# DoRA forward kernel: row stores moved to ScalarE's DMA ring, with a small zero store ahead of them

## The chip, the cores and the metric

The kernel runs on one core of a Trainium2 chip. A core has engines that run side by side: TensorE (PE, matrix products; PEld is its loading of weights), VectorE (DVE), ScalarE (ACT), GpSimd (POOL) and SyncE (SP). Sixteen DMA engines move data between the chip's main memory and the core's on-chip memory. An engine of the core issues a transfer into a ring (a queue); SP has one ring and ACT has another, and both feed the same 16 DMA engines. Times are device microseconds (us) of one execution.

## What is computed

The reference builds one 256 x 256 weight matrix and multiplies 32,768 rows by it:

```
W_adapted = W + scale * (lora_A @ lora_B)
W_norm = np.sqrt(np.sum(W_adapted ** 2, axis=0, keepdims=True) + 1e-8)
W_final = (W_adapted / W_norm) * m
y = x.reshape(-1, 256) @ W_final
```

x has the shape (16, 2048, 256) in float32, 33.5 MB, and y is as large. The rank of lora_A and lora_B is 16. All of W, lora_A, lora_B and m is 289 KB.

## The kernel before

The rows are cut into 8 blocks of 4,096 rows (`BLK`, 4 MB each). A block lies in one buffer `x_sb` of 128 partitions, with 32 rows on each, so that every partition reads 32 KB in one piece. There are 5 such buffers (`XBUFS`).

First the small inputs are loaded: W (`w_nat`, L65) on SP's ring, and lora_A (`a_nat`, L63), lora_B (`b_nat`, L67) and m (`m_row`, L69) on ACT's ring. From them the final weights `w_final` are made in bfloat16 (L85 to L129) by a chain of short steps over PE, DVE and ACT.

Then each block goes through 8 groups of 4 rows per partition. In a group PE transposes the rows through the identity (L156, tile `xt_ps`), DVE casts the result to bfloat16 (L162, `xt_sb`), PE multiplies by `w_final` (L167, `y_ps`), and ACT copies the product back over the same rows of `x_sb` (L174). When the groups of a block are done, one store of 4 MB writes the block out (L179); the last block is stored in three parts, of 2, 1 and 1 MB (`store_after`).

All loads and stores of rows are issued by SP, in the order in which they are written in the code, because `manual_schedule` holds SP's order fixed. That order is: W, loads 0 to 4, store 0, store 1, load 5, store 2, load 6, store 3, load 7, stores 4 to 6, and the three parts of store 7. Load 5 goes into the buffer of block 0 and so waits until store 0 has landed; loads 6 and 7 wait for stores 1 and 2. A store waits for ACT's last copy of its block. As SP works its list in order, what stands behind a waiting transfer waits too, and on the ring the transfers are worked in the order of issue.

Of the kernel before, what the change touches and what calls it, by code (L numbers as in the profile page):

```python
# [11 lines left out]
def kernel(  # L12
# [10 lines left out]
    nc = tc.nc  # L23
    P = 128
    FP32 = mybir.dt.float32
# [9 lines left out]
    KC = IN // P  # L35
    J = 4
    DJ = 32
    XBUFS = 5
    BLK = DJ * P
    NBLK = N // BLK  # L40

# [1 line left out]

    consts = ctx.enter_context(tc.tile_pool(name="consts", bufs=1))
    startup = ctx.enter_context(tc.tile_pool(name="startup", bufs=1))
    xpool = ctx.enter_context(tc.tile_pool(name="xpool", bufs=XBUFS))
    xtpool = ctx.enter_context(tc.tile_pool(name="xtpool", bufs=2))
    pp_xt = ctx.enter_context(tc.tile_pool(name="pp_xt", bufs=2, space=bass.MemoryType.PSUM))
    pp_y = ctx.enter_context(tc.tile_pool(name="pp_y", bufs=2, space=bass.MemoryType.PSUM))
# [1 line left out]
    def load_x(b):  # L51
        t = xpool.tile([P, DJ, IN], FP32, name="x_sb", tag="x_sb")
        nc.sync.dma_start(
            out=t,
            in_=x_flat[b * BLK : (b + 1) * BLK].rearrange("(p j) k -> p j k", p=P),
        )
        return t

    ctx.enter_context(tc.manual_schedule(engines={mybir.EngineType.SP}))


    a_nat = startup.tile([P, KC, R], FP32)
    nc.scalar.dma_start(out=a_nat, in_=lora_A.rearrange("(c p) r -> p c r", p=P))  # L63
# [3 lines left out]
    nc.scalar.dma_start(out=b_nat, in_=lora_B)  # L67
    m_row = startup.tile([1, OUT], FP32)
    nc.scalar.dma_start(out=m_row, in_=m[None, :])  # L69

    identity = consts.tile([P, P], FP32)
    make_identity(nc, identity)
# [10 lines left out]
    with tc.high_priority():  # L83
# [15 lines left out]
        for c in range(KC):  # L99
# [10 lines left out]
            out=wa, in0=ab_ps, scalar=float(scale), in1=w_nat, op0=ALU.mult, op1=ALU.add  # L110
# [27 lines left out]
    store_after = [[CH] for _ in range(NBLK)]  # L138
    store_after[-1] = [CH // 2, 3 * CH // 4, CH]

    x_tiles = {}
    for b in range(XBUFS):
        x_tiles[b] = load_x(b)

    for b in range(NBLK):
        x_sb = x_tiles[b]
        j_stored = 0


        for c in range(DJ // J):
            xt_ps = pp_xt.tile([P, KC, J * P], FP32, tag="psxt", name="xt_ps")
            for j in range(J):
                for kc in range(KC):
                    nc.tensor.transpose(  # L156
                        xt_ps[:, kc, j * P : (j + 1) * P],
                        x_sb[:, c * J + j, kc * P : (kc + 1) * P],
                        identity,
                    )  # L160
            xt_sb = xtpool.tile([P, KC, J * P], BF16, name="xt_sb")
            nc.vector.tensor_copy(out=xt_sb, in_=xt_ps)  # L162

            y_ps = pp_y.tile([P, J, OUT], FP32, tag="psy", name="y_ps")
            for kc in range(KC):
                for j in j_order:
                    nc.tensor.matmul(  # L167
                        y_ps[:, j, :],
                        xt_sb[:, kc, j * P : (j + 1) * P],
                        w_final[:, kc, :],  # L170
                        start=(kc == 0 and (j % (J // 2)) == 0),
                        stop=(kc == KC - 1 and (j % (J // 2)) == (J // 2) - 1),
                    )
            nc.scalar.copy(out=x_sb[:, c * J : (c + 1) * J, :], in_=y_ps)  # L174

            if c + 1 in store_after[b]:
                j0 = j_stored
                j_stored = (c + 1) * J
                nc.sync.dma_start(  # L179
                    out=out_flat[b * BLK : (b + 1) * BLK].rearrange(  # L180
                        "(p j) k -> p j k", p=P
                    )[:, j0:j_stored, :],
                    in_=x_sb[:, j0:j_stored, :],
                )
        if b >= 1 and b - 1 + XBUFS < NBLK:
            x_tiles[b - 1 + XBUFS] = load_x(b - 1 + XBUFS)


# [33 lines left out]
```

## Time and profile before

| what | value |
|---|---|
| median of 4 runs | 165.67 us (165.36 to 165.73) |
| the profiled execution's own time | 165.29 us |
| its span (first to last instruction) | 163.5 us |
| busy: DVE cast L162 | 75.4 us, 64 of 1.219 us |
| busy: ACT copy L174 | 64.8 us, 64 of 1.013 us |
| 4 MB row loads, issue to landing (median of 8) | 29.5 us |
| 4 MB row stores, issue to landing (median of 7) | 28.5 us |
| main memory read and written | 33.85 MB and 33.55 MB, 412 GB/s over the span |

The profile is of one execution. Its busy table says how long each engine worked. A line of slices cuts the span into 40 equal parts and gives the busy share of each in tenths, 9 being 90% or more. The DMA part lists the rings by number (q1 is SP's, q10 is ACT's, q8 and q14 fetch instructions): packets, MB, and the time that their packets took as a share of 16 engines' span. A stretch line gives for a window of time each engine's busy us (and number of instructions), the clock that TensorE was granted, the DMA engines' busy share and the GB/s; as a packet counts where it starts, shares of a short window can go a little past 1. A line of waits reads "who <- for whom: us in total, times, longest". The chain of waits follows the last instruction back to what released it. Besides, the trace holds a record of each DMA packet: its start, its length and its ring; a 4 MB transfer is 128 packets of 32 KB, one for each partition, and 8 for each DMA engine.

### The profile page before, as it was taken

How to read it: one execution, taken by the hardware profiler on the slowest of the kernel's cores; microseconds unless marked ns; L12 is line 12 of the kernel's file. 1: busy time of each engine (PE TensorE's matmuls, PEld its weight loads, DVE VectorE, ACT ScalarE, POOL GpSimd, SP SyncE). 2: the span in 40 equal slices, each digit the busy share in tenths (PEclk: the TensorE clock that was granted, in tenths of full speed). 3: DMA queues.
4: the chain of work that ended last, by engine and by line, in shares of the span. 5: the costliest groups of instructions: out<-in, count | busy, mean ns of one | idle time of the engine just before them, and what ended most of it. 6: DMA issues, size and time to landing. Idle time of an engine off the chain costs nothing.

```text
span 163.5 us, 2378 instructions
## 1 busy us (share of the span) xinstructions
PE 123.7 (76%) x1034; PEld 108.0 (66%) x1034; DVE 81.1 (50%) x76; ACT 66.8 (41%) x67; POOL 0.7 (0%) x6
## 2 busy tenths in 40 slices
PE   0149788888888888888888888888888888884000
PEld 0028677777777777777777777777777777772000
DVE  0145755555555555555555555555555555551000
ACT  3001144444444444444444444444444444444000
POOL 1000000000000000000000000000000000000000
PEclk9999999999999999999999999999999999999755
DMA  6998998998999999999999999999999999999992
GB/s 196 429 473 385 457 441 381 489 409 385 493 401 361 401 469 417 427 449 413 433 433 409 477 409 417 433 427 421 441 425 457 421 417 441 425 421 429 405 407 106
DMA packets 3180, 67.55 MB, mean 413 GB/s; under 512 B 593, under 2 KB 866, under 8 KB 866
## 3 DMA queue, kind: packets, MB, share of 16 engines
q1 hardware_dynamic: 2864, 67.37, 96.8%
q8 instruction: 8, 0.13, 0.3%
q10 hardware_dynamic: 306, 0.03, 0.2%
q14 instruction: 2, 0.02, 0.0%
HBM read 33.85 MB, written 33.55 MB: 412 GB/s over the span
## 4 chain that ended last, share of the span: by engine, by line
PE 55%; DVE 26%; DMA 4%; issue 4%; ACT 1%; DVEq 1%; ACTq 1%
PE y_ps L167 35%; DVE xt_sb L162 23%; PE xt_ps L156 17%; DMA m_row<-in_m_dram 4%; PE n_ps L118 1%; DVE rnorm L127 1%; DVEq L217 1%; PE mb_ps L94 1%; ACT x_sb L174 1%; DVE w_final L129 0%; DVE sq L113 0%; DVE wa L109 0%; ACTq L63 0%; ACTq L67 0%; ACT norm L122 0%
## 5 line engine op out<-in xcount | busy, mean ns | idle before, releaser
L162 DVE CAST xt_sb<-xt_ps 128x1024 bf16<-128x1024 f32 x64 | 75.4, 1219 | 55.2 <-PE xt_ps L156 55.2
L174 ACT COPY x_sb<-y_ps 128x1024 f32<-128x1024 f32 x64 | 64.8, 1013 | 70.4 <-PE y_ps L167 69.8
L167 PE MATMUL y_ps<-w_final,xt_sb 128*128 128x256 bf16 x512 | 66.7, 273 | 15.3 <-DVE xt_sb L162 14.9
L156 PE MATMUL xt_ps<-identity,x_sb 128*128 128x128 f32 x512 | 67.2, 277 | 0.0
L167 PEld LDWEIGHTS <-xt_sb 128*128 128x128 bf16 x512 | 46.8, 98 | 28.3 <-DVE xt_sb L162 23.9
L156 PEld LDWEIGHTS xt_ps<-identity,x_sb 128*128 128x128 f32 x512 | 59.3, 144 | 1.0 <-DMA x_sb<-in_x_dram 0.3
L122 ACT ACTIVATE norm<-n_ps,eps_col 128x256 f32<-128x256 f32 x1 | 0.5, 474 | 10.5 <-PE n_ps L118 10.5
L94 PE MATMUL mb_ps<-m_row,ones 1*128 1x256 f32 x2 | 1.2, 694 | 4.5 <-DMA m_row<-in_m_dram 4.5
L94 PEld LDWEIGHTS mb_ps<-m_row,ones 1*128 1x128 f32 x2 | 0.5, 304 | 5.0 <-issue 5.0
L89 PE MATMUL aT_ps<-identity,a_nat 128*16 128x128 f32 x2 | 0.6, 397 | 4.0 <-DMA a_nat<-in_lora_A_dram 4.0
L118 PE MATMUL n_ps<-sq,ones 128*128 128x256 f32 x4 | 2.1, 674 | 1.5 <-DVE sq L113 1.5
L85 DVE CAST b_bf<-b_nat 16x256 bf16<-16x256 f32 x1 | 0.3, 281 | 5.6 <-DMA b_nat<-in_lora_B_dram 5.6
L127 DVE RECIPROCAL rnorm<-norm 128x256 f32<-128x256 f32 x1 | 1.8, 1755 | 2.0 <-ACT norm L122 2.0
L89 PEld LDWEIGHTS aT_ps<-identity,a_nat 128*16 128x16 f32 x2 | 0.1, 88 | 4.0 <-issue 4.0
L118 PEld LDWEIGHTS n_ps<-sq,ones 128*128 128x128 f32 x4 | 1.2, 324 | 2.2 <-DVE sq L113 2.0
L79 ACT ACT_TABLE_LOAD x1 | 1.3, 1283 | 2.3 <-issue 2.3
L96 DVE COPY m_all<-mb_ps 128x256 f32<-128x256 f32 x1 | 0.4, 426 | 3.1 <-PE mb_ps L94 3.1
L129 DVE TENSOR_TENSOR w_final<-wam,rnorm 128x256 bf16<-128x256 f32 x2 | 0.8, 421 | 0.0
L125 DVE TENSOR_TENSOR wam<-wa,m_all 128x256 f32<-128x256 f32 x2 | 0.8, 418 | 0.0
L113 DVE TENSOR_TENSOR sq<-wa 128x512 f32<-128x512 f32 x1 | 0.7, 692 | 0.0
L109 DVE SCALAR_TENSOR_TENSOR wa<-ab_ps,w_nat 128x512 f32<-128x512 f32 x1 | 0.7, 692 | 0.0
L100 PE MATMUL ab_ps<-b_bf,aT 16*128 16x256 bf16 x2 | 0.6, 416 | 0.0
(11 smaller groups left out, 2.0 us busy)
## 6 DMA issues: line engine op xcount, KB each, us to landing
x_sb<-in_x_dram SPq DMA_DIRECT2D x8, 4096.0 KB, 29.5
out_dram<-x_sb SPq DMA_DIRECT2D x7, 4096.0 KB, 28.5
out_dram<-x_sb SPq DMA_DIRECT2D x1, 2048.0 KB, 15.7
out_dram<-x_sb SPq DMA_DIRECT2D x2, 1024.0 KB, 12.5
w_nat<-in_W_dram SPq DMA_DIRECT2D x1, 256.0 KB, 3.0
a_nat<-in_lora_A_dram ACTq DMA_DIRECT2D x1, 16.0 KB, 3.1
b_nat<-in_lora_B_dram ACTq DMA_DIRECT2D x1, 16.0 KB, 5.3
m_row<-in_m_dram ACTq DMA_DIRECT2D x1, 1.0 KB
```

The lines of the kernel that those rows point to most:

```text
L79: nc.scalar.activation(out=warm, in_=eps_col, func=AF.Sqrt)
L89: nc.tensor.transpose(aT_ps[:, c * P : (c + 1) * P], a_nat[:, c, :], identity)
L94: nc.tensor.matmul(mb_ps, ones[0:1, :], m_row, start=True, stop=True)
L118: nc.tensor.matmul(n2_ps, ones, sq[:, c, :], start=(c == 0), stop=(c == KC - 1))
L125: nc.vector.tensor_mul(out=wam[:, c], in0=wa[:, c], in1=m_all)
L127: nc.vector.reciprocal(out=rnorm, in_=norm)
L129: nc.vector.tensor_mul(out=w_final[:, c], in0=wam[:, c], in1=rnorm)
L156: nc.tensor.transpose(xt_ps[:, kc, j * P : (j + 1) * P], x_sb[:, c * J + j, kc * P : (kc + 1) * P], identity,)
L162: nc.vector.tensor_copy(out=xt_sb, in_=xt_ps)
L167: nc.tensor.matmul(y_ps[:, j, :], xt_sb[:, kc, j * P : (j + 1) * P], w_final[:, kc, :], start=(kc == 0 and (j % (J // 2)) == 0), stop=(kc ...
L174: nc.scalar.copy(out=x_sb[:, c * J : (c + 1) * J, :], in_=y_ps)
L217: with _tile.TileContext(nc) as tc:
```

## The change

The row stores are issued by ACT instead of SP, so that they go to ACT's ring, and SP's ring holds W and the row loads alone. SP's order is no longer written out by hand: the loads stand in the block loop, and each is issued as soon as its buffer is free (there are 5 buffers, as before). A tile `mark` of 128 x 16 zeros is made by a DVE memset, and ACT stores it (8 KB, 64 bytes from each partition) to a scratch tensor in main memory, behind its three small loads. Nothing reads the scratch tensor.

```diff
-    ctx.enter_context(tc.manual_schedule(engines={mybir.EngineType.SP}))
...
     nc.scalar.dma_start(out=m_row, in_=m[None, :])
+    scratch = nc.dram_tensor("scratch", (P, 16), FP32, kind="Internal").ap()
+    mark = startup.tile([P, 16], FP32)
+    nc.vector.memset(mark, 0.0)
+    nc.scalar.dma_start(out=scratch, in_=mark)
...
-    x_tiles = {}
-    for b in range(XBUFS):
-        x_tiles[b] = load_x(b)
     for b in range(NBLK):
-        x_sb = x_tiles[b]
+        x_sb = load_x(b)
...
-                nc.sync.dma_start(
+                nc.scalar.dma_start(
                     out=out_flat[b * BLK : (b + 1) * BLK].rearrange(
                         "(p j) k -> p j k", p=P
                     )[:, j0:j_stored, :],
                     in_=x_sb[:, j0:j_stored, :],
                 )
-        if b >= 1 and b - 1 + XBUFS < NBLK:
-            x_tiles[b - 1 + XBUFS] = load_x(b - 1 + XBUFS)
```

More of the change, by code (lines that the diff above doesn't have):

```diff
@@ L37 @@
     DJ = 32
-    XBUFS = 5
     BLK = DJ * P
@@ L45 @@
     startup = ctx.enter_context(tc.tile_pool(name="startup", bufs=1))
-    xpool = ctx.enter_context(tc.tile_pool(name="xpool", bufs=XBUFS))
+    xpool = ctx.enter_context(tc.tile_pool(name="xpool", bufs=5))
     xtpool = ctx.enter_context(tc.tile_pool(name="xtpool", bufs=2))
```

## The prediction

> **What bounds the kernel now.** I read the busy table first, then the DMA part, the slices, the stretches, and last who waited for whom on the queue that issues.
>
> ```profile
> PE 123.7 (76%) x1034; PEld 108.0 (66%) x1034; DVE 81.1 (50%) x76; ACT 66.8 (41%) x67; POOL 0.7 (0%) x6
> ...
> DMA  6998998998999999999999999999999999999992
> ...
> q1 hardware_dynamic: 2864, 67.37, 96.8%
> q8 instruction: 8, 0.13, 0.3%
> q10 hardware_dynamic: 306, 0.03, 0.2%
> ```
>
> No compute engine is above 76%, while the 16 DMA engines are full from the first slice to the last. q1 is SyncE's ring (67.37 MB, 96.8% of 16 engines' span); q10 is ScalarE's, which today carries 0.03 MB. The chain of waits names PE and DVE, since it follows back from the last instruction, but that instruction is not the end of the work. The stretches show it (columns: PE, PEld, DVE, ACT, POOL busy, clock, DMA share, GB/s):
>
> ```profile
> 4.00:12.00 8.00, 2.20 (x6) 0.88 (x6) 2.27 (x5) 0.00 (x0) 0.00 (x0) 1.00 1.03 436
> ...
> 45.30:49.30 4.00, 3.56 (x33) 3.17 (x32) 2.36 (x2) 1.91 (x3) 0.00 (x0) 1.00 0.92 393
> 49.30:52.30 3.00, 2.55 (x24) 2.23 (x23) 2.11 (x2) 1.17 (x2) 0.00 (x0) 1.00 1.09 360
> 52.30:56.30 4.00, 3.55 (x34) 3.17 (x32) 2.24 (x3) 2.03 (x2) 0.00 (x0) 1.00 1.01 434
> ...
> 152.00:158.00 6.00, 0.00 (x0) 0.00 (x0) 0.00 (x0) 0.00 (x0) 0.00 (x0) 0.63 0.99 421
> 158.00:163.50 5.50, 0.00 (x0) 0.00 (x0) 0.00 (x0) 0.00 (x0) 0.00 (x0) 0.50 0.42 176
> ```
>
> After 152 us nothing computes and DMA still runs at 0.99. The last store is issued at about 150.1 us (ACT's last copy starts at 149.05 and takes 1.01) and lands 12.5 us later, at 162 us: it stands behind the ring's backlog. So the end is bytes over rate. The trace's packet records give the rate: each of the 1,920 packets of 32 KB has a median of 1.213 us, that is 27.0 GB/s for an engine, and on each engine the next starts where the last ends. A 4 MB transfer is 8 such packets on each engine, 9.7 us. The 16 engines finish between about 159.3 and 162.2 us; the last sets the end. The queue's own waits:
>
> ```profile
> SPq L179 <- ACT x_sb L174: 99.6, 10, 20.3
> SPq L53 <- DMA out_dram<-x_sb: 31.7, 3, 14.1
> ```
>
> SP waits 99.6 us for copies and 31.7 us for stores to free a buffer, but as the ring always held 10 us or more of earlier work, none of it left the engines idle.
>
> **The change, part by part.**
>
> 1. Bytes. 67.37 MB on q1 become about 33.8 MB on q1 and 33.55 MB on q10, plus 8 KB. On the same 16 engines that is the same 128 packets' worth of 1.213 us for each engine, 155.3 us. What is left to ask is whether an engine is ever idle, and whether a packet becomes longer.
>
> 2. Idle turns. Only SP's order changes: loads 5, 6 and 7 no longer stand behind stores 1, 2 and 3. The five first loads start at 3.1 us as before. Stores are issued as blocks end, by the records at 34.2, 50.7, 67.1, 83.6 and so on, 16.46 apart. By 34.2 some 26 of the 40 first load packets of an engine are through ((34.2 - 3.1) / 1.213). From then the rings share. If they take turns, a load and a store packet take 2.43 us, so store 0 ends at about 55, store 1 at 74, store 2 at 94, store 3 at 113; the 38 load packets left (14 and 24 of loads 5 to 7) end at 34.2 + 38 x 2.43 = 126.5. Load 5 may start at 56, when load 4 still has until 68; load 6 at 75, load 5 lasting to 88; load 7 at 95, load 6 lasting to 107. So a load is always ready, and a store is always ready from 34 on. At 126.5 some 26 store packets are left, 31.5 us: 158. No turn is empty: cost 0. What covers it is the 16.46 us pitch of the blocks being shorter than the 19.4 us of a shared store.
>
> 3. Compute. Block 5 begins at 99.7 (17.4 + 5 x 16.46), load 5 lands at 89; block 6 at 116.1 against 108; block 7 at 132.6 against 128. Cost 0, with 4 us to spare at the tightest; even a late block 7 costs nothing until it ends some 7 us after today's 150 (162.2 - 150.1 less about 4 for the last 1 MB alone, an estimate from 8 packets of 0.309 us and 1.1 us from the first issue to the first packet).
>
> 4. ScalarE. It issues 10 stores. One is 0.33 us on SP, 0.49 to 0.53 on ACT for the small loads. Behind each stands the next copy. Stores follow an odd group, and after an odd group ACT idles 1.90 us (after an even one 0.19), so 0.53 is hidden; uncovered it would be 5.3 us in all, and then only of compute's slack. The early issue waits for DVE's memset (0.06 to 0.17 us by the two memsets there) and delays the table load from 2.34 by half a us; ACT's next work is at 14.32 after 10.49 us of idling. Cost 0.
>
> 5. The 8 KB store is 8 rows of 64 bytes and a completion on each engine, 9 turns on q10 behind m_row. Nothing reads it. Each turn falls between two load packets and costs what part 6 prices; the trace has no 64-byte store. Bounds: a 64-byte load packet takes 11 ns (0.1 us for nine); by the completions' 48 ns of part 6, 0.4 us. I take 0.1. It moves load 0, which lands at 13.9, by that; the first cast waits for w_final until 17.38 anyway.
>
> The Trainium skill speaks against this store: "DMA: Bandwidth & Descriptors", Specifications, says that below 512 B a transfer is read, modified and written. No run here shows such a store, and with no price there the sum by it stays open above 0.1.
>
> 6. Ring switches, the disputed term. Today an engine changes from a load to a store only between transfers, and at 81 to 84 and 91 to 94, where some engines still ran one and others the next, packets kept 1.213 to 1.216. So mixing directions is free; changing rings at each packet is what is new. The nearest rows are the small loads of q10 beside the x loads. They show the turns: b_nat's packets at 4.35 to 4.69, its completions at 5.62 to 5.93, m_row at 7.19, its completion at 8.45, one for each x packet. In the chain:
>
> ```profile
> 1.77 7.18 DMA m_row<-in_m_dram
> ```
>
> one KB took 7.18 us, since it waited for turns. The x packet behind a 1 KB q10 packet was longer than 1.213 by a median of 12 ns (mean 45, 0 to 268, 16 cases); behind a completion by a median of 48. Behind an instruction fetch of 16 KB (q8) an x packet took 1.6 to 1.76, 0.5 longer, but that data goes to an engine's program store. Per engine 38 load packets follow a store packet: 38 x 12 ns = 0.46 us; by the mean, and with the store packets paying as well, 2 x 38 x 45 ns = 3.4 us. Below nothing it could be by 0.5 us: the stretch from 49.3 to 52.3, just where the first store's packets come up, moved 360 GB/s instead of 434 (3 us x 17%). I take 0.46, since a 1 KB packet is data, as a store packet is.
>
> The Trainium skill, same page, "Queues, rings and completion order", has an engine drain some 9 to 17 descriptors of a ring before it turns to the next. The records above show one. By the page a store's 8 packets would go together, with an eighth of the switches: 0.06 instead of 0.46.
>
> **Sum.** 165.29 (the profiled run, span 163.5) + 0.46 + 0.1 = 165.9. The median of the runs is 165.67, 0.38 above the profiled one, so 166.3 there: 0.4% slower. Below 0.2% (0.33 us) this measurement can't tell a change from none.
>
> **Rivals.**
>
> A. Faster. The dip at 49.3 to 52.3 is a price of the first write through a ring, and the small store pays it early, on small packets. Place: the first store packets on all 16 engines. By the records most engines lost 0.4 to 0.9 us there, and some of those that end last 1.5. For: it stands once, at the first store; later changes from load to store are free, but for a smaller one at 100 to 102. Against: the long packets are the last two of load 4, not those of store 0, whose first ones took 1.213. Price 0.5 to 1.5, so 164.2 to 165.2, say 164.8. It decides if a switch costs less than 13 ns (0.5 / 38).
>
> B. Switches cost the mean or more, on both rings: 165.67 + 3.4 = 169.1. For: completions' 48 ns, and the 0.5 us behind the fetches. Against: 11 of the 16 packets behind 1 KB show 19 ns or less.
>
> C. Nothing, 165.7: the rings are drained in bursts, or a load's reads run on while a store's packet goes out, and 128 packets remain 128 packets.
>
> D. Loads starve compute: stores take more than their turn, load 7 lands 8 us or more after 132.6, and the last store goes out late. Every us beyond is a us at the end; 170 or more. Against: the turns of q10 in the first 9 us are one to one.
>
> **Chances.** Forecast (166.0 to 167.5) 0.36; A 0.30; C 0.15; B 0.13; D or worse 0.06. Slower by over 0.2%: forecast, B and D, 0.54 (some of the forecast falls within); same 0.16; faster 0.30. The range reaches from A's lower end to B's sum with the small store at its dearest (0.4): 164.2 to 169.5. The forecast's own range is 166.0 to 167.5.
>
> **What would show it.** In the profile after: q1 and q10 near 48% each, together 97%; DMA 9 in all slices to the last; x packets of 1.22 to 1.23 in the shared stretch (34 to 127) if right, 1.213 if C, 1.26 and more if B; GB/s there about 1% below 434. Loads 5 to 7 issued near 56, 75 and 95, the last copy still near 150. A dip at the first store, near 35 us, speaks against A, its absence for A. The prediction is wrong if the slices show DMA below 9 in the middle (an empty turn), or a copy that ends past 157.

## The result and the profile after

The changed kernel takes 165.22 us (median of 35 runs, 164.94 to 165.64) where the kernel before takes 165.71 (57 runs, 165.29 to 166.24). The ratio is 0.997, with a 95% interval of 0.9964 to 0.9975: faster by 0.49 us, where I forecast slower by 0.4%. A repetition of both (below) gave 0.9992 with an interval of 0.9981 to 1.0003, which reaches past 1. So the gain is 0.3% in the one comparison and 0.1% or nothing in the other.

The DMA view of the changed kernel (slices; rings with packets, MB, share; one issue with its us to landing):

```profile
DMA  5999998999999999999999999999999999999992
...
q1 hardware_dynamic: 1424, 33.82, 48.8%
q10 hardware_dynamic: 1890, 33.60, 48.0%
q8 instruction: 8, 0.13, 0.3%
...
scratch<-mark ACTq DMA_DIRECT2D x1, 8.0 KB, 16.0
```

The bytes are halved between q1 and q10, the sum of the shares stays at 97%, and no slice is empty. The stretches (PE, PEld, DVE, ACT, POOL busy, clock, DMA share, GB/s):

```profile
30.90:34.90 4.00, 3.55 (x33) 3.17 (x32) 2.24 (x3) 2.02 (x2) 0.00 (x0) 1.00 1.03 442
34.90:38.40 3.50, 3.48 (x32) 3.09 (x30) 1.74 (x2) 2.02 (x2) 0.00 (x0) 1.00 1.09 356
...
40.00:120.00 80.00, 71.37 (x614) 62.49 (x615) 44.77 (x38) 38.40 (x39) 0.00 (x0) 1.00 1.00 431
152.00:158.00 6.00, 0.00 (x0) 0.00 (x0) 0.00 (x0) 0.00 (x0) 0.00 (x0) 0.76 1.00 426
158.00:163.50 5.50, 0.00 (x0) 0.00 (x0) 0.00 (x0) 0.00 (x0) 0.00 (x0) 0.50 0.39 164
```

The dip that stood at 49.3 to 52.3 stands now at 34.9 to 38.4, where store 0 joins the loads (issued at 33.9). From 40 to 120, with both rings in use, the engines move 431 GB/s at a share of 1.00. The waits of SP's queue:

```profile
SPq L52 <- DMA out_dram<-x_sb: 83.7, 3, 45.8
```

SP now waits 83.7 us for three stores, 45.8 of them for store 0, instead of 31.7, and it costs nothing, as loads 5 to 7 are still issued early enough (at 59.7, 79.4 and 98.4).

The profiled execution of after took 165.27 us with a span of 163.5. That of before took 165.29 with the same span, as low as the lowest of its kernel's 57 runs. So this pair of profiles can't show where 0.49 us went. I needed more profiles of both, and a finer reading.

**The finer reading.** The packet records carry no engine number, but on each DMA engine a packet starts within some ns of the end of the one before, so that 16 lines can be followed through the span (where two engines' packets end together, two lines can be swapped; I used the count of 8 packets for each transfer to keep them apart). Three things delay a line beyond its packets' 1.213 us each:

- A fetch of instructions (8 in a span, at about 28, 45, 61, 77, 94, 111, 128 and 145 us) costs the one engine that it falls on 1.3 to 1.57 us.
- One engine has 45 to 51 store packets of about 1.265 us, 2.3 to 2.7 us in all, in either kernel.
- The dip, once, on all engines: 0.77 us on average in before, 0.94 in after.

Most engines with none of the first two end at 159.1 to 159.6; the others end at up to 160.3, mostly after one more loss of 0.4 to 0.8 us that I can't explain. The execution's time is the end of the last line plus 3.0 to 3.2 us, in every profile of the table. "Lost at the turn" is what the two engines that the fetches near 28 and 45 us hit lose in the dip. c_before, c_before2 and after2 are the two kernels run again, e_markonly and e_nomark the first two experiments below.

| kernel (rings) | slow-store engine ends | early-fetched engines lose at the turn | and end at | last line | profiled time |
|---|---|---|---|---|---|
| before (one) | 162.08 | 1.46, 1.48 | 162.18, 162.23 | 162.23 | 165.29 |
| c_before (one) | 161.91 | 1.80, 1.83 | 162.05, 162.01 | 162.05 | 165.15 |
| e_markonly (one) | 162.08 | 1.85, 1.74 | 162.50, 162.10 | 162.50 | 165.51 |
| c_before2 (one) | 161.99 | 1.47, 1.44 | 162.78, 162.60 | 162.78 | 165.89 |
| after (two) | 162.11 | 0.60, 0.98 | 160.63, 160.91 | 162.11 | 165.27 |
| after2 (two) | 162.24 | 0.57, 1.33 | 160.69, 161.08 | 162.24 | 165.38 |
| e_nomark (two) | 162.46 | 1.11, 0.86 | 161.20, 160.79 | 162.46 | 165.65 |

On one ring the two early-fetched engines pay 1.4 to 1.85 us at the turn, where those in step pay mostly 0.4 to 1.1; in c_before2 they lose another 1.2 near 100 and 121 us, at the later turns from loads to stores. So in these four profiles they are the last, past the slow-store engine, by 0.1 to 0.8. On two rings they pay like the others and are through 1.0 to 1.7 us before the slow-store engine, which alone sets the end. (In after2 the line of the first fetch runs side by side with another from 71 to 81 us, so that it may end at 160.69 or at 161.20.)

This shows which engine is last, but not the whole gain. The last line ends at 162.39 on average in the four profiles on one ring and at 162.27 in the three on two: 0.12 us, where the medians differ by 0.49. The slow-store engine itself ends later on two rings (162.1 to 162.5, against 161.9 to 162.1 on one), and the times of these profiles are alike, 165.46 on average and 165.43. In the two other one-ring profiles with the same order of stores (p_one_late and p_one_lag15, below) the early-fetched engines end 0.2 to 0.6 us before the slow-store engine. c_before2, at 165.89, stands just above the upper quartile of the 57 runs of before (165.86).

### The profile page after: what moved, and what is told of

It is laid out like the page before. It is cut to its first block, busy times and chain, and to the rows that moved or that the text cites. A ratio compares the mean times of both kernels' runs of the same rounds, so it can differ in the third digit from the quotient of the medians.

```text
span 163.5 us, 2373 instructions
## 1 busy us (share of the span) xinstructions
PE 124.4 (76%) x1034; PEld 107.1 (66%) x1034; DVE 81.1 (50%) x77; ACT 66.0 (40%) x67; POOL 0.7 (0%) x6
## 4 chain that ended last, share of the span: by engine, by line
PE 57%; DVE 26%; DMA 4%; issue 2%; ACT 1%; DVEq 1%; ACTq 1%
PE y_ps L165 33%; DVE xt_sb L160 23%; PE xt_ps L154 22%; DMA m_row<-in_m_dram 4%; PE n_ps L122 1%; DVE rnorm L131 1%; DVEq L213 1%; PE mb_ps L98 1%; ACT x_sb L172 1%; DVE w_final L133 0%; DVE sq L117 0%; DVE wa L113 0%; ACTq L64 0%; ACTq L60 0%; ACT norm L126 0%
## 5 line engine op out<-in xcount | busy, mean ns | idle before, releaser
L172 ACT COPY x_sb<-y_ps 128x1024 f32<-128x1024 f32 x64 | 64.1, 1013 | 72.5 <-PE y_ps L165 72.4
L165 PE MATMUL y_ps<-w_final,xt_sb 128*128 128x256 bf16 x512 | 65.5, 273 | 12.6 <-DVE xt_sb L160 12.5
L165 PEld LDWEIGHTS <-xt_sb 128*128 128x128 bf16 x512 | 47.8, 98 | 23.8 <-DVE xt_sb L160 19.1
L154 PEld LDWEIGHTS xt_ps<-identity,x_sb 128*128 128x128 f32 x512 | 57.8, 142 | 7.8 <-DVE xt_sb L160 6.7
```

Source lines behind the costliest of these rows:

```text
L154: nc.tensor.transpose(xt_ps[:, kc, j * P : (j + 1) * P], x_sb[:, c * J + j, kc * P : (kc + 1) * P], identity,)
L165: nc.tensor.matmul(y_ps[:, j, :], xt_sb[:, kc, j * P : (j + 1) * P], w_final[:, kc, :], start=(kc == 0 and (j % (J // 2)) == 0), stop=(kc ...
```

## The experiments

**What each part of the change does.** Four kernels, compared on one chip. c_before is the kernel before, unedited; e_onering is the changed kernel with the first edit below and `nc.sync` for the row stores.

```diff
# e_nomark: from the changed kernel
-    scratch = nc.dram_tensor("scratch", (P, 16), FP32, kind="Internal").ap()
-    mark = startup.tile([P, 16], FP32)
-    nc.vector.memset(mark, 0.0)
-    nc.scalar.dma_start(out=scratch, in_=mark)
# e_markonly: the same four lines added to the kernel before
```

> The kernel before, unchanged, as a control and for a second profile. Both theories: ratio 1.000, median near 165.7. The profile of before was of a run at 165.29, the low end of its 57 runs, and that of after ran 165.27, so the pair of profiles shows no difference; this one, if it is of a typical run, should show the last of the 16 DMA engines ending 0.3 to 0.6 us later than 162.23, and on which engine, in which stretch, that was lost.

> The changed kernel without the zero store (no scratch tensor, no memset). Theory R, two rings: the gain is of splitting loads and stores over two rings, the small store does nothing; then ratio to before 0.997, median 165.2. Theory M, the small store: it pays early for a part of what the first store costs; then the gain goes, ratio 1.000, median 165.7, and the dip in the loads at the first store (34.9 to 38.4 us, about 1 us on each engine with the small store) grows by 0.3 us or more.

> The kernel before with the 8 KB zero store added behind the small loads on ScalarE's ring; row loads and stores all stay on SyncE's ring in the fixed order. Theory R: ratio 1.000 (by the price that I put on the small store 0.1 us more, 1.0006). Theory M: ratio 0.997, and the dip at 49.3 to 52.3 is smaller by 0.3 us or more.

> The changed kernel without the zero store and with the row stores on SyncE again, in the order that Tile chooses and not by hand: W, loads 0 to 2, store 0, store 1, load 3, store 2, load 4 and so on. So only the hand-written order is taken away. Both theories agree here: loads 3 and 4 wait behind stores that wait for compute, so that the ring runs dry: load 2 is through at 32, store 0 comes at 34.2 and is through at 45, store 1 comes at 50.7, load 3 at 51 to 71, 8 to 10 us of empty turns before load 3 and more behind it, so 175 to 185 us. If it stays at 165 to 166, the order matters for nothing.

Measured: c_before 0.9986 (0.9972 to 1.0001), e_nomark 0.9975 (0.9962 to 0.9988), e_markonly 0.9982 (0.9967 to 0.9996), e_onering 1.1511 (1.1478 to 1.1545).

Without the small store the gain is all there (165.25 against 165.22), and the dip is no larger: 1.01 us on average against 0.94 with it. With the small store alone on the old ring 0.9982 can't be told from the control's 0.9986, and its early-fetched engines still lose 1.85 and 1.74. So the gain does not need the 8 KB store. That the store does nothing at all is not shown, as the interval of e_markonly overlaps that of e_nomark too. The profile of c_before is again of a low run (165.15).

e_onering shows what the hand-written order was for. The page's DMA part, and who SP waits for:

```profile
DMA  7999997792299999999479999999829989892695
...
q1 hardware_dynamic: 2864, 67.37, 86.2%
```

```profile
SPq L173 <- ACT x_sb L168: 143.8, 10, 20.3
SPq L173 <- DMA x_sb<-in_x_dram: 32.2, 4, 11.2
```

Tile, the layer that schedules the instructions where the order is not written out, issued loads 0 to 2, then store 0, store 1, load 3 and so on, one load behind each store. Loads that could run stand behind stores that wait for ACT's copies (143.8 us instead of 99.6), and the slices with 2, 4 and 6 are the ring run dry. I expected 175 to 185 us; it took 190.96, as the empty turns come back at later blocks. Two rings need no order by hand, since a waiting store holds up no load.

**When the turn comes.** I first thought that its place was what mattered (theory E): before the second fetch, fewer engines are behind. f_early puts store 0 ahead of load 4 on one ring; g_late holds store 0 back on two. Beside them, h_k15 relieves one DMA engine and i_bigmark makes the small store 1 MB.

```diff
# f_early: kernel before, first loads and block loop
-    for b in range(XBUFS):
+    for b in range(XBUFS - 1):
         x_tiles[b] = load_x(b)
...
+        if b == 0:
+            x_tiles[XBUFS - 1] = load_x(XBUFS - 1)
# g_late: e_nomark with ScalarE's order by hand, and stores gathered
+    ctx.enter_context(tc.manual_schedule(engines={mybir.EngineType.Activation}))
...
+                held.append((b, x_sb, j0, j_stored))
+                if b >= 1:   # issue all that is held, then clear
# h_k15: e_nomark, the two last stores
+                if b == NBLK - 1 and j0 > 0:
+                    parts = [(0, 120), (120, P)]
# i_bigmark: the changed kernel
-    scratch = nc.dram_tensor("scratch", (P, 16), FP32, kind="Internal").ap()
+    scratch = nc.dram_tensor("scratch", (P, 2048), FP32, kind="Internal").ap()
```

> The kernel before, all on SyncE's ring in a fixed order, with one place changed: store 0 is issued before load 4 and not behind it. Theory E (when the first store comes): the dip at the first store costs 0.6 to 1.0 us on an engine that is in step and 1.5 to 1.85 on one that an instruction fetch (about 28 and 45 us) has put 1.5 us behind; two such engines are among the last in all three one-ring profiles (162.0 to 162.5). With store 0 behind load 3 the dip comes at 39 to 43 us, ahead of the second fetch, at most one engine is late, and only the engine with slow stores ends past 162: ratio 0.997 on one ring. Theory R (two rings as such): one ring stays at 1.000.

> Two rings without the zero store, ScalarE's order written out by hand, and store 0 held back until block 1 is done too, so that stores 0 and 1 are issued together at 50.7 us. Theory E: the dip comes at 50 to 55 us, behind the second fetch, late engines pay double again and the gain goes: ratio 0.999 to 1.000. Theory R: the rings still alternate from 50 us on, ratio 0.997. No engine idles in either: five loads last until 52, and load 5 comes at about 62, when store 0 has landed and store 1 is under way.

> Two rings without the zero store; each of the two last 1 MB stores is cut into one of 120 partitions and one of 8. A guess of mine on the division is to be tested: 120 partitions go to 15 DMA engines, 8 each, the other 8 to 8 engines, one each, so that one engine is relieved of 4.85 us (16 packets of 0.303 to 0.309), and 8 engines get 0.62 more. In each profile one engine has some 50 store packets of 1.265 instead of 1.213 us and ends last or nearly so (161.9 to 162.5); the others with a fetch end at 160.6 to 161.2. If the relieved engine is that one, the end falls to 161.3 to 161.8, 0.5 to 1 us, ratio to the kernel before 0.991 to 0.994. If it is among the 8 that get more, 1.001; if among the rest, 0.997 as without the cut.

> The changed kernel with a store of 1 MB of zeros (8 KB from each partition) instead of 8 KB. It adds 2.4 us of packets. Rival A in its stronger form (a real store on this ring pays the first write early): the dip at 35 to 38 us goes, and one shows between 4 and 20 us instead. Against A: the dip at the first row store stays at about 1 us on each engine. Time by the bytes 167.6 to 168.0 (ratio 1.012 to 1.015), 1 us less if the dip goes and does not come back elsewhere.

Measured: f_early 1.0041 (1.0025 to 1.0057), g_late 0.9955 (0.994 to 0.997), h_k15 1.0078 (1.0049 to 1.0107), i_bigmark 1.0113 (1.0096 to 1.013).

Theory E fell with f_early, which is slower: its early-fetched engines end at 163.21 and 162.78, the slow-store engine at 162.09. The dip near 41 us is mild on average (0.39), but the engine of the first fetch loses 1.41 there, and both lose again later: 1.5 us in all from 82 to 102 for the one, 0.74 near 61 and 1.3 near 101 for the other. So it seemed that the loss at a turn on one ring goes with an engine that is behind, wherever the turn is. This is theory L below. g_late says less: its 0.9955 speaks against E, but the repetition below gave 0.9998, which is what E expected, and in the first profile of g_late the engine of the first fetch ends level with the slow-store engine (161.88 and 161.87).

h_k15 shows that my division was right: one line has 124 packets' worth of 32 KB instead of 128 and ends at 154.79, eight have 128.5. The slow-store engine was among the eight, and ends at 162.68. But packets of the last stores, 0.31 us each, took up to 0.5 us longer near 155 to 160, which none did in e_nomark, and the last line is another at 162.96. So I lost where I wanted to win; which engine is slow, other than that it is one of those eight, is open. The profiled execution (165.93) was the fastest of six, with a median of 166.84.

i_bigmark, the stretches that answer to those of after:

```profile
34.90:38.40 3.50, 3.05 (x29) 2.66 (x27) 2.36 (x2) 1.60 (x2) 0.00 (x0) 1.00 1.04 449
38.40:42.40 4.00, 3.51 (x30) 3.04 (x29) 2.36 (x2) 1.05 (x2) 0.00 (x0) 1.00 1.02 393
```

The loads are 2.4 us later, so the dip comes at 38.4 to 42.4, and it is half as deep: 0.45 us on average instead of 0.94. But the loads lost more earlier: the load packets that start before 26 us took 0.61 us more for each engine than 1.213 each, against 0.08 in after and 0.37 in after2, and 0.23 of that lies at 5 to 7 us, just ahead of the first packet of the 1 MB store (7.1). (f_early, without such a store, lost 0.54 there, so this too may be chance.) So a store of that size may pay for half the dip early, but no gain is left: the time is 167.41, 1.75 above the kernel before in the same set and 2.2 above the changed kernel's 165.22, for 2.4 us of packets. A store of 8 KB leaves the dip as it was.

**Is it the lag?** Theory L: on one ring an engine that is behind pays more at a turn. Extra loads into one partition of the fifth buffer (overwritten by load 4) put one DMA engine behind; in the first pair by three packets.

```diff
# p_one_late: kernel before (p_two_late: the same with nc.scalar for the row stores)
     for b in range(XBUFS):
-        x_tiles[b] = load_x(b)
+        x_tiles[b] = load_x(b, first[b])
+        if b == 1:
+            for p in range(3):
+                nc.sync.dma_start(
+                    out=first[4][p : p + 1],
+                    in_=x_flat[p * DJ : (p + 1) * DJ].rearrange("(p j) k -> p j k", p=1),
+                )
```

> The kernel before with three extra loads of 32 KB behind load 1, each into one partition of the fifth buffer, which load 4 overwrites later. If a transfer of one partition goes to one DMA engine, that engine is put 3.64 us (3 x 1.213) behind the rest. Theory L (an engine that lags pays again): on one ring an engine that is behind loses more at the turn from loads to stores (1.5 to 1.85 us against 0.6 to 0.9 for an engine in step, with a lag of 1.5), and at later turns too, and so the last engine is one of the lagging ones in some executions; on two rings it pays no more than the others. Then here the delayed engine ends at 159.2 + 3.64 + 1.2 or more = 164.0 or later, 1.8 us or more past the last engine of before: ratio 1.010 or more. Theory N (the dip is spread by chance, a lag costs just itself): 159.2 + 3.64 = 162.8, 0.6 past: ratio 1.003 to 1.005. A fetch or the slow stores on the same engine would add 1.4 or 2.5 in both; the trace tells.

> The same three extra loads in the two-ring form (row stores on ScalarE's ring, no zero store, SyncE's order as before). Both theories: the delayed engine ends at 159.2 + 3.64 = 162.8, its loss at the first store no greater than the others' (about 1 us, which is in the 159.2): ratio 1.001 to 1.003. If it comes out as late as in the one-ring form (within 0.3 us), theory L falls.

> The kernel before once more, as the control of this call and for a third profile of it: ratio 1.000. Theory L: in the profile the engines that were hit by the fetches at about 28 and 45 us lose 1.4 us or more in the dip near 50 us, the others 0.5 to 1.0, and the last engine is one of those two, or the one with slow stores.

Measured: p_one_late 1.0034 (1.0021 to 1.0046), p_two_late 1.0051 (1.0036 to 1.0066), c_before2 1.0001 (0.9991 to 1.0012).

One line does have 131 packets' worth instead of 128 in each, so a transfer of one partition does go to one engine. But it ends at 163.22 on one ring and at 163.92 on two: the delayed engine lost 1.11 us at the turn on one ring, little more than engines in step there (0.6 to 1.1), while the early-fetched engines of the same execution lost 1.43 and 1.55. For a lag of 3.64 us theory L is wrong, and two rings were, if anything, worse: at the first store 1.17, and from 82 to 117 us another 0.7 in small pieces. c_before2 gave the fourth one-ring profile of the table.

**The same with the fetch's own lag.** One extra packet and a quarter (1.52 us), and the changed kernel and g_late once more beside them.

```diff
# p_one_lag15, p_two_lag15: as p_one_late and p_two_late, with
-            for p in range(3):
+            for p, rows in ((0, DJ), (1, DJ // 4)):
                 nc.sync.dma_start(
-                    out=first[4][p : p + 1],
+                    out=first[4][p : p + 1, 0:rows],
```

> One ring, fixed order, with extra loads of 32 KB and of 8 KB into one partition each behind load 1, so that one DMA engine is 1.52 us behind (1.213 + 0.309), as a fetch puts it (1.3 to 1.57). Theory L2 (a lag of one packet and a part is what costs at the turn): that engine loses 1.4 to 1.85 us near 51 us, as the two engines with early fetches do, and ends at 159.2 + 1.5 + 0.8 = 161.5 or later. Theory F (something of the fetch itself costs): it loses 0.5 to 1.1 like engines in step and ends at 160.7 to 161.0, and only the two fetched engines lose 1.4 or more. Time in both: ratio 0.999 to 1.003, since other engines end at 162 and later anyway.

> The same extra loads with the row stores on ScalarE's ring. Both theories: no engine pays for its lag, the delayed engine loses 0.5 to 1.2 us near 35 us and ends at 160.7 to 161.0; the engine with slow stores is the last at 161.9 to 162.5; ratio 0.996 to 0.998. If the delayed or a fetched engine loses 1.4 or more here too, the second ring is not what spares them.

> The changed kernel unchanged: ratio 0.997 again. Its last engine is the one with slow stores (161.9 to 162.5), and the engines with fetches at about 28 and 45 us end between 160.5 and 161.5.

> Two rings with store 0 held back to 50.7 us, once more, beside the changed kernel on one chip. If holding it back is worth something of itself (in its first profile the engine with slow stores lost 0.64 us at the turns and not 0.9), ratio 0.995 to 0.996 and 0.1 to 0.3% below the changed kernel; if the first result was chance, 0.997.

Measured: p_one_lag15 0.9997 (0.9988 to 1.0006), p_two_lag15 0.9987 (0.9975 to 0.9998), after2 0.9992 (0.9981 to 1.0003), g_late2 0.9998 (0.9982 to 1.0014).

Here the delayed engine, which no fetch hit, lost 1.69 us at 51.0 on one ring, beside 1.76 and 1.81 on the two early-fetched ones and 0.8 to 1.4 on the rest. On two rings it lost 0.97 near 35 us, and the early-fetched ones 0.91 and 0.93. By this pair, one profile of each kernel, it is the lag of about 1.5 us, and not the fetch, that costs extra at the turn on one ring, and the second ring spares it there.

But what was spared did not all last. On two rings the delayed engine and the engine of the first fetch each lost another 0.8 us in small pieces between 59 and 120 us. They end at 161.46 and 161.74, where on one ring they end at 161.73 and 161.75; only the engine of the second fetch keeps its gain (160.42 instead of 161.69). The slow-store engine is the last in both, at 162.48 on two rings and 162.09 on one. Why 3.64 us of lag cost no extra is open; a lag of whole packets may matter, or one so long that the others' turn is over, and no run tells these apart.

After2 gained less, 0.15 us (165.26 against 165.41). The changed kernel's medians stand at 165.22 and 165.26, those of before at 165.71, 165.55, 165.66, 165.74 and 165.41 in the five sets. They differ by 0.33 us for one and the same kernel, so that only comparisons within a set count. The quartiles of after are closer together (165.09 and 165.27 in its 35 runs) than those of before (165.52 and 165.86 in its 57). That would fit the table: the slow-store engine ends within 0.6 us in its seven profiles, while the early-fetched engines, the last on one ring there, end anywhere from 162.0 to 162.8. g_late, which looked better than both at first, came back at 0.9998: no version is shown to beat the changed kernel. The profile of g_late2 shows well that the last engine sets the time and not the mean: its 16 lines end at 161.5 on average instead of 160.3 in after, but the last one at 162.29 instead of 162.11, and it took 165.49 us instead of 165.27.

## Why the prediction was wrong, point by point

- **Bytes, idle turns, compute, ScalarE** (parts 1 to 4): right. 97% over two rings, no empty slice, loads 5 to 7 issued at 59.7, 79.4 and 98.4 (I had 56, 75 and 95), the last copy at 150.1, a store 0.34 us on ACT and hidden.
- **The 8 KB store** (part 5, 0.1 us): too small to be seen; without it the time is 165.25 instead of 165.22. Its packets took 11 ns, the x packets behind them 1.213 us.
- **Ring switches** (part 6, 0.46 us): this step failed. Load packets in the shared stretch (40 to 126 us) have a median of 1.213 us. Their mean is 1.2136 without the few that took over 1.3 us and 1.2155 with them, so 38 of them cost 0.02 to 0.09 us, not 0.46; in after2 0.04 to 0.15. The row that I sized it by was not a price of switching: in after, x packets behind a 1 KB packet were 4 ns longer on average and not 45, behind a completion mostly 0 and not 48; in after2 the mean behind 1 KB is about 70, by three packets, with a median of 1. Small differences in the first 9 us vary from one execution to the next, and I took those of one for a law. That b_nat's and m_row's packets took turns with x packets was read rightly: load packets of one engine start 2.42 us apart in the shared stretch. The other half of this step, that a change between loads and stores on one ring is free, held for most engines and not for those that lag: near 100 us the two last lines of before lost 0.65 and 0.43 us.
- **The sum** was made for an average engine, though my own first part said that the last of the 16 sets the end. I never asked which one is last, and by what. With switches and store at nothing the sum gives 165.7, and the time is another 0.5 us below that. Here the table shows a change: on two rings the early-fetched engines pay 0.7 us less at the turn on average, and the last line moves from them (162.0 to 162.8) to the slow-store engine (162.1 to 162.5). In these profiles that makes 0.12 us; where the rest comes from is not shown.
- **Rival A** named the nearest time (164.8) for a wrong reason: the dip stayed, 0.94 us with the small store and 1.01 without. **Rival C** had the reason right for the packets, that 128 remain 128, and missed the time by 0.5 us. B and D did not come: no dearer packets, no late block.

The Trainium skill's rule in "DMA: Bandwidth & Descriptors", Queues, rings and completion order, that an engine drains some 9 to 17 descriptors before it changes rings, is not what these runs show for packets of 32 KB: a store's 8 packets and the loads' went one by one.

What stays open: how much of the gain comes from the change of the last engine, what the dip at the first meeting of stores and loads is (it slows load packets ahead of the first store packet), why a lag of 1.5 us makes it dearer on one ring and costs in small pieces on two, and why one engine is slow at stores.

## What to carry to other kernels

When 16 DMA engines are full from end to end, the time is that of the last engine: look for what makes one engine later than the rest (instruction fetches, one engine's slow stores, a turn from loads to stores), not for the mean rate. Loads and stores on two rings alternate packet by packet at next to no cost (0.02 to 0.15 us for the loads here), need no order by hand, and here spared the lagging engines an extra loss at the first turn; on one ring a wrong order cost 15%. A profile at the edge of its kernel's runs can hide a difference as small as this one: take several before explaining it.

## What the runs showed of the hardware that I had not expected

- One of the DMA engines takes 1.265 us for a 32 KB store packet where the others take 1.213, in every profile that I followed, which puts it 2.3 to 2.7 us behind. For a load packet in the changed kernel it takes 1.213 before the stores begin, like the others, and about 1.22 beside them.
- A 16 KB instruction fetch costs the engine that it falls on 1.3 to 1.57 us, more than twice the 0.61 us of a 16 KB store packet.
- A 1 MB store early on ScalarE's ring went with half the later dip (0.45 instead of 0.94 us) and with larger losses of the loads ahead of it; one of 8 KB left the dip.
